# First feed-forward matrix by quarter blocks: seven products for eight, float32 gated values, and a second matrix that runs over eight PSUM banks

## Chip, cores and metric

The kernel runs on one core of a Trainium2 chip. The metric is the device time of one execution in microseconds (us), the median of several runs. TensorE (PE) multiplies, VectorE (DVE), ScalarE (ACT) and GpSimd (POOL) do elementwise work, and SyncE (SP) issues most of the DMAs. Operands lie in SBUF; PE writes to PSUM, which has eight banks of 128 x 512 float32.

## What is computed

One decoder layer on x of 512 tokens x 1024 features, all in float32. Three attention mixers are gated, merged, sent through `w_out` and added to x. Then comes the feed-forward block, which is what the change rewrites:

```python
h = _rms(x, norm2_g[layer])                                   # 512 x 1024
gate, up = jnp.split(h @ w_ffn_in[layer], 2, axis=-1)         # w_ffn_in 1024 x 5632
x = x + (jax.nn.silu(gate) * up) @ w_ffn_out[layer]           # w_ffn_out 2816 x 1024
```

## The kernel before

**Float32 products as three matmuls.** Every operand is split in two: `split` (L80) lets ACT round it to a "hi" part (L81) and DVE, or POOL where `eng` says so, subtract that from the operand to get a "lo" part (L82). `mm3` (L103) then issues hi x hi, hi x lo and lo x hi into one PSUM tile (L106 to L108). `weights` (L84) loads 256 KB blocks of a weight matrix through SP's queue into `raw` (five buffers), and splits each block into `whi` and `wlo` (six buffers each, of 128 x 512). It does this at high priority: the scheduler that sets the order on every engine places these instructions as early as buffers allow.

**Output projection (L1053 to L1080).** `w_out` is handled in four column blocks of 256; for each, four token tiles get eight `mm3`. DVE adds the PSUM tile to the residual `x2` (L1072). `x2`, four tiles of 512 KB, is loaded a second time from HBM for this (L1043). In the last column block, `norm_T` normalises each token tile, transposes it on PE and splits it to `xh2` and `xl2`.

**First feed-forward matrix (L1082 to L1129).** The loop over `c` goes through 11 chunks of 256 gate columns and the 256 up columns that go with them. In a chunk, each of two groups `j` of 128 columns gets eight `mm3` for gate and eight for up, with all 512 tokens as the moving operand: 2 x 2 x 8 x 3 = 96 matmuls of 128x512. The first chunk is done in halves of 256 tokens, since the last token tiles' norms are still under way. ACT takes the tanh (L1121), DVE multiplies twice (L1122, L1123), both times reading a PSUM tile, and the result is split at once to `hh` and `hl`.

**Second feed-forward matrix (L1130 to L1145).** Two halves of 512 output columns one after the other; in each, 22 blocks of 128 rows of `w_ffn_out` are multiplied with the 22 pairs `hh`, `hl` for four token tiles, in four PSUM banks. The last three blocks (`LAST`) are done tile by tile, so that the sums and the writes to HBM follow each other.

PSUM tiles `pf` of this part come from one pool of eight banks (`m2_tile`) in rotation.

Of the kernel before, what the change touches and what calls it, by code (L numbers as in the profile page):

```python
# [67 lines left out]
def block_kernel(ctx: ExitStack, tc: tile.TileContext, x, norm1_g, norm2_g, w_in, qk_norm_g, cmp_pos, cmp_w,  # L68
                 w_ba, w_bb, w_bc, w_out, w_fi, w_fo, rel_bias, onehot, masks, out):
    nc = tc.nc  # L70
    x, out = x[0], out[0]
    w_in, w_ba, w_bb, w_bc, w_out, w_fi, w_fo = (w[0] for w in (w_in, w_ba, w_bb, w_bc, w_out, w_fi, w_fo))
# [3 lines left out]
    wp = ctx.enter_context(tc.tile_pool(name="wts", bufs=6))  # L76
# [3 lines left out]
    def split(dst_hi, dst_lo, src, eng=None):  # L80
        nc.scalar.copy(dst_hi, src)  # L81
        (eng or nc.vector).tensor_tensor(out=dst_lo, in0=src, in1=dst_hi.bitcast(F32), op=ALU.subtract)  # L82

    def weights(w, segs, kcs, per=2, pool=()):  # L84

        res = {}
        width = sum(n for _, n in segs)
        with tc.high_priority():
            for k0 in kcs[::per]:
                raw = wp.tile([128, per, width], F32, name="raw", tag="raw", bufs=5)  # L90
                o = 0
                for c0, n in segs:
                    nc.sync.dma_start(raw[:, :, o:o + n],
                                      w[k0 * 128:(k0 + per) * 128, c0:c0 + n].rearrange("(k p) c -> p k c", p=128))
                    o += n
                hi = wp.tile([128, per, width], F32R, name="whi", tag="whi")
                lo = wp.tile([128, per, width], F32R, name="wlo", tag="wlo")
                split(hi, lo, raw, nc.gpsimd if pool and k0 // per % 4 in pool else None)
                for j in range(per):
                    res[k0 + j] = (hi[:, j, :], lo[:, j, :])  # L100
        return res

    def mm3(ps, pairs, k0=0, n=None):  # L103
        n = n or len(pairs)
        for j, ((ah, al), (bh, bl)) in enumerate(pairs, k0):
            nc.tensor.matmul(ps, ah, bh, start=(j == 0), stop=False)  # L106
            nc.tensor.matmul(ps, ah, bl, start=False, stop=False)  # L107
            nc.tensor.matmul(ps, al, bh, start=False, stop=(j == n - 1))  # L108
# [58 lines left out]
    def norm_T(xt, t, ss, n, g, xh, xl, pst, tmp, lo):  # L167
# [940 lines left out]
    for c in range(0, DFF, 256):
        if c:
            wg = weights(w_fi, [(c, 256)], list(range(KC)))  # L1110
            pgs = [m2_tile() for _ in range(2)]
# [4 lines left out]
        for j in range(2):
            pu = pus[j]
            if c:
                ffn_in(pu, wu, j)
            th = hp_.tile([128, S], F32, name="fth", tag="fth", bufs=2)  # L1120
            nc.scalar.activation(th, pgs[j], AF.Tanh, scale=0.5)  # L1121
# [8 lines left out]
    for c in range(0, D, 512):  # L1130
        pss = [m2_tile() for _ in range(NT)]
        wk = {}
        for k in range(NF):
            wk.update(weights(w_fo, [(c, 512)], [k], per=1))
            for t in range(NT if k < NF - LAST else 0):
                ts = slice(t * 128, (t + 1) * 128)
                mm3(pss[t], [((hh_[k][:, ts], hl_[k][:, ts]), wk[k])], k, NF)
        for t in range(NT):
            ts = slice(t * 128, (t + 1) * 128)
            mm3(pss[t], [((hh_[k][:, ts], hl_[k][:, ts]), wk[k]) for k in range(NF - LAST, NF)], NF - LAST, NF)  # L1140
            for q, dma in enumerate((nc.sync, nc.scalar)):
                cs = slice(256 * q, 256 * q + 256)
                xs = x2[t][:, c + 256 * q:c + 256 * q + 256]
                nc.vector.tensor_tensor(out=xs, in0=xs, in1=pss[t][:, cs], op=ALU.add)
# [20 lines left out]
```

## Time and profile before

| what | value |
|---|---|
| median of 3 runs | 999.03 us (994.99 to 999.38) |
| profiled execution | 995.54 us, span of its instructions 993.8 us |
| granted TensorE clock, mean | 0.993 |
| PE / DVE / ACT / POOL busy | 974.3 / 568.1 / 437.5 / 175.4 us |
| output projection | about 576 to 624 us of the span |
| first feed-forward matrix | about 624 to 867 us |
| second feed-forward matrix | about 867 us to the end |

The table's busy times are unions of the instructions' spans on each engine. Matmuls overlap in the pipeline, so a matmul's own duration is longer than the distance from its start to the next start; that distance is what a stream of matmuls costs. The stages follow each other on PE, so a stage's length is read off the first starts of its matmuls. From 648 us on POOL has no instruction.

### The profile page before, as it was taken

What the parts mean: (1) busy time and instruction counts of PE and PEld (TensorE: products, weight loads), DVE (VectorE), ACT (ScalarE), POOL (GpSimd) and SP (SyncE); (2) the same over time, 40 slices, a digit from 0 to 9 for tenths busy, and PEclk for the clock granted to TensorE, in tenths of its full rate; (3) what the DMA queues carried; (4) which work ended last, traced back from release to release, by engine and by line L of the source; (5) the groups of instructions that cost most, each with busy time, mean ns of one, the idle gap of its engine ahead of it and who ended that gap; (6) DMA issues with size and microseconds to landing.
All of it is one profiled execution on the core that took longest, in us unless ns stands there. A gap on an engine that the chain in (4) does not pass through costs nothing.

```text
span 993.8 us, 16076 instructions
## 1 busy us (share of the span) xinstructions
PE 974.3 (98%) x5887; PEld 827.0 (83%) x5887; DVE 568.1 (57%) x1277; ACT 437.5 (44%) x956; POOL 175.4 (18%) x156
## 2 busy tenths in 40 slices
PE   6999999999999999989999999999999999999998
PEld 6889999899887578858777899988888888888886
DVE  6699999766665655665764654544344444422321
ACT  5544555755665555554543434433233233322220
POOL 4135555543100202231110312000000000000000
PEclk9999999999999899989999999999999999999999
DMA  8541344433232334346613462233333323332421
GB/s 210 122 128 44 85 119 132 123 109 122 90 104 67 85 117 138 107 141 193 180 62 97 140 210 86 85 94 108 96 85 105 107 85 91 110 97 96 138 75 42
DMA packets 119264, 109.91 MB, mean 111 GB/s; under 512 B 19931, under 2 KB 105234, under 8 KB 119186
## 3 DMA queue, kind: packets, MB, share of 16 engines
q1 hardware_dynamic: 116994, 107.85, 37.4%
q10 hardware_dynamic: 2192, 1.05, 0.4%
q8 instruction: 46, 0.75, 0.3%
q14 instruction: 32, 0.26, 0.1%
HBM read 96.66 MB, written 12.21 MB: 110 GB/s over the span
## 4 chain that ended last, share of the span: by engine, by line
PE 96%; DMA 1%; DVE 1%; ACT 1%; issue 0%; SPq 0%; DVEq 0%; ACTq 0%
PE pf L108 14%; PE pf L107 14%; PE pf L106 14%; PE pm L107 13%; PE pm L106 13%; PE pm L108 13%; PE tr L111 5%; PE ovb L541 2%; PE lg L363 2%; PE lg L364 2%; PE ova L541 1%; PE lg L843 1%; DMA raw<-in_w_in 1%; PE ovc L888 1%; PE lg L838 0%
## 5 line engine op out<-in xcount | busy, mean ns | idle before, releaser
L82 DVE TENSOR_TENSOR wlo<-raw,whi 128x512 fp32r<-128x512 f32 (+1 forms) x243 | 182.5, 756 | 147.7 <-ACT whi L81 146.6
L81 ACT CAST whi<-raw 128x512 fp32r<-128x512 f32 (+1 forms) x288 | 176.8, 619 | 173.9 <-PE pf L108 78.6
L107 PE MATMUL pm<-wlo,xh 128*128 128x256 f32 (+1 forms) x512 | 145.9, 288 | 0.3 <-DVE wlo L82 0.3
L108 PE MATMUL pm<-whi,xl 128*128 128x256 f32 (+1 forms) x512 | 145.3, 286 | 0.5 <-POOL xl L82 0.5
L106 PE MATMUL pm<-whi,xh 128*128 128x256 f32 (+1 forms) x512 | 145.7, 289 | 0.0
L107 PE MATMUL pf<-xl,whi 128*128 128x512 f32 (+1 forms) x384 | 142.6, 372 | 0.1
L106 PE MATMUL pf<-xh,whi 128*128 128x512 f32 (+1 forms) x384 | 142.5, 372 | 0.0
L108 PE MATMUL pf<-xh,wlo 128*128 128x512 f32 (+1 forms) x384 | 142.0, 371 | 0.0
L107 PEld LDWEIGHTS pm<-wlo,xh 128*128 128x128 f32 x512 | 98.5, 193 | 1.9 <-issue 0.8
L108 PEld LDWEIGHTS pm<-whi,xl 128*128 128x128 f32 x512 | 98.7, 193 | 1.4 <-POOL xl L82 0.8
L106 PEld LDWEIGHTS pm<-whi,xh 128*128 128x128 f32 x512 | 98.3, 194 | 0.4
L107 PE MATMUL pm<-xl,whi 128*128 128x512 f32 x224 | 88.8, 396 | 0.0
L108 PE MATMUL pm<-xh,wlo 128*128 128x512 f32 x224 | 88.6, 395 | 0.0
L106 PE MATMUL pm<-xh,whi 128*128 128x512 f32 x224 | 88.4, 395 | 0.0
L107 PEld LDWEIGHTS pf<-xl,whi 128*128 128x128 f32 x384 | 72.3, 188 | 12.8 <-DVE xl L82 0.3
L108 PEld LDWEIGHTS pf<-xh,wlo 128*128 128x128 f32 x384 | 72.2, 188 | 12.6
L106 PEld LDWEIGHTS pf<-xh,whi 128*128 128x128 f32 x384 | 72.2, 188 | 12.3
L82 POOL TENSOR_TENSOR wlo<-raw,whi 128x512 fp32r<-128x512 f32 x45 | 62.2, 1402 | 111.6 <-ACT whi L81 100.8
L106 PE MATMUL pf<-whi,hh 128*128 128x512 f32 x176 | 69.4, 395 | 0.0
L108 PE MATMUL pf<-whi,hl 128*128 128x512 f32 x176 | 69.4, 395 | 0.0
L107 PE MATMUL pf<-wlo,hh 128*128 128x512 f32 x176 | 69.4, 395 | 0.0
L562 ACT ACTIVATE p<-p,m 128x128 f32<-128x128 f32 (+3 forms) x96 | 53.9, 562 | 28.6 <-DVE m L547 26.4
(312 smaller groups left out, 1702.3 us busy)
## 6 DMA issues: line engine op xcount, KB each, us to landing
raw<-in_w_in SPq DMA_DIRECT2D x92, 256.0 KB, 3.0
raw<-in_w_ffn_in SPq DMA_DIRECT2D x88, 256.0 KB, 2.9
raw<-in_w_ffn_out SPq DMA_DIRECT2D x44, 256.0 KB, 2.8
raw<-in_w_in SPq DMA_DIRECT2D x52, 128.0 KB, 2.4
x<-in_x SPq DMA_DIRECT2D x8, 512.0 KB, 5.9
tab<-dvec SPq DMA_DIRECT2D x16, 256.0 KB, 3.3
dz<-tz SPq DMA_DIRECT2D x16, 256.0 KB, 2.4
tz<-dz SPq DMA_DIRECT2D x16, 256.0 KB, 3.3
```

The source lines that it names most:

```text
L81: nc.scalar.copy(dst_hi, src)
L82: (eng or nc.vector).tensor_tensor(out=dst_lo, in0=src, in1=dst_hi.bitcast(F32), op=ALU.subtract)
L106: nc.tensor.matmul(ps, ah, bh, start=(j == 0), stop=False)
L107: nc.tensor.matmul(ps, ah, bl, start=False, stop=False)
L108: nc.tensor.matmul(ps, al, bh, start=False, stop=(j == n - 1))
L111: nc.tensor.transpose(dst, src, ident[0:src.shape[0], 0:src.shape[0]])
L363: nc.tensor.matmul(lg, qs, k[:, 0, 0:w], start=True, stop=False)
L364: nc.tensor.matmul(lg, qs, k[:, 1, 0:w], start=False, stop=stop)
L541: mm = nc.tensor.matmul(ov[64 * j:64 * j + 64, 128 * b:S], v(b), pts[j][:, 4 * b:3 * b + NT, :], start=first and b == 0, stop=last and b = ...
L562: nc.scalar.activation(p[:, 0:w], p[:, 0:w], AF.Exp, bias=m[:, 0:1], scale=-1.0, accum_out=m[:, 1:2])
L843: nc.tensor.matmul(lg[32 * r:32 * r + 32, c:c + n], ld["q", g][hp, 128 * i + 32 * r:128 * i + 32 * r + 32], ld["k", g][hp, 128 * r:128 * r ...
L888: nc.tensor.matmul(ov[h, 128 * b_:128 * q1], ld["v", 0][:, b_, h], d["pt", jj][:, 2 * b_:b_ + q1, :], start=b_ == 0, stop=False)
```

## The change

The chunks after the first are computed by quarter blocks with a Strassen scheme in Winograd's form. For a chunk, the weight block is cut in four: `a11` (upper 512 rows, gate columns), `a21` (upper rows, up columns), `a12` (lower rows, gate), `a22` (lower rows, up), each of two 128 x 512 tiles. The normalised input is cut in four by feature half and token half. Seven products of such quarters, with sums of quarters as operands, replace eight.

- `norm_T` also copies the normalised input in float32 to `xf` (ACT, 128x512, eight times). Four differences of its quarters (`t1` to `t4`, 128 x 1024 each) are made on DVE and split, once.
- Weight blocks go through SP to a pool of their own, `fraw` (twelve buffers). The sums `s1` to `s4` are made on POOL, eight adds of 128x512 a chunk, in `fsum` or in place. Seven operands of two tiles are split, fourteen tiles a chunk in place of eight; POOL subtracts two of the lo parts, DVE twelve.
- A product is 2 x 4 x 3 = 24 matmuls of 128x256. A chunk has 7 x 24 = 168 of them, in place of 96 of 128x512.
- Products are summed outside PSUM: one ACT copy and seven DVE adds of a PSUM tile to a float32 tile in SBUF (`ea`, `eu1`, `eu2`, `ec22`). `swiglu` then reads SBUF alone, where the two multiplies read PSUM before.
- The gated values stay in float32 (`hid`) and are split only in the second matrix, block by block. There the row block is the outer loop and both column halves run together over eight banks.

```diff
+    xf = np_.tile([128, KC, S], F32, name="xf")          # norm_T: nc.scalar.copy(xf[:, 4*q:4*q+4, ts], ps)
...
+    for name, out_, p, q in (("t1", f11, f12, f11), ("t3", f12, f22, f12), ("t2", f22, f22, f11), ("t4", f21, f21, f22)):
+        th_, tl_ = (tp.tile([128, HK, S // 2], F32R, name=f"x{name}{v}") for v in "hl")
+        nc.vector.tensor_tensor(out=out_, in0=p, in1=q, op=ALU.subtract)
+        split(th_, tl_, out_)
+        xb[name] = (th_, tl_)
...
+    def swiglu(dst, g, u):
+        th = ep.tile([128, 512], F32, name="fth", tag="fth", bufs=2)
+        nc.scalar.activation(th, g, AF.Tanh, scale=0.5)
+        nc.vector.scalar_tensor_tensor(out=th, in0=th, scalar=1.0, in1=g, op0=ALU.add, op1=ALU.mult)
...
+        nc.vector.scalar_tensor_tensor(out=dst, in0=th, scalar=0.5, in1=u, op0=ALU.mult, op1=ALU.mult)
...
+    def fi_operands(c):
+        fr = {}
+        with tc.high_priority():
+            for r, (n, k) in enumerate((("a11", 0), ("a21", 0), ("a22", HK), ("a12", HK))):
+                for h in range(2):
+                    t_ = ep.tile([128, 2, 256], F32, name="fraw", tag="fraw", bufs=12)
+                    k0, c0 = k + 2 * h, c + (DFF if n[1] == "2" else 0)
+                    nc.sync.dma_start(t_, w_fi[k0 * 128:k0 * 128 + 256, c0:c0 + 256].rearrange("(k p) c -> p k c", p=128))
+                    fr[n, h] = t_
+        def add(n, dst, p, q, op):
...
+                nc.gpsimd.tensor_tensor(out=fr[n, h], in0=fr[p, h], in1=fr[q, h], op=op)
+        def get(n):
+            with tc.high_priority():
+                if n == "s2":
+                    add("s1", None, "a21", "a22", ALU.add)
+                    add("s2", None, "s1", "a11", ALU.subtract)
+                elif n == "s3":
+                    add("s3", "a21", "a11", "a21", ALU.subtract)
+                elif n == "s4":
+                    add("s4", "s2", "a12", "s2", ALU.subtract)
+                res = []
+                for h in range(2):
+                    hi = wp.tile([128, 2, 256], F32R, name="whi", tag="whi")
+                    lo = wp.tile([128, 2, 256], F32R, name="wlo", tag="wlo")
+                    split(hi, lo, fr[n, h], nc.gpsimd if (n, h) in (("a22", 1), ("s1", 1)) else None)
+                    res += [(hi[:, j, :], lo[:, j, :]) for j in range(2)]
+            return res
...
+    for c in range(256, DFF, 256):
+        get = fi_operands(c)
...
+        for a, b in (("a11", "b11"), ("s2", "t2"), ("a12", "b21"), ("s3", "t3"), ("s1", "t1"), ("a22", "t4"), ("s4", "b22")):
+            w, (bh, bl) = get(a), xb[b]
+            ps = m2_tile()
             for j in range(2):
+                cs = slice(128 * j, 128 * j + 128)
+                mm3(ps[:, 256 * j:256 * j + 256], [((w[k][0][:, cs], w[k][1][:, cs]), (bh[:, k, :], bl[:, k, :]))
+                                                   for k in range(HK)])
+            if a == "a11":
+                nc.scalar.copy(ev["a"], ps)
+            elif a == "s2":
+                add_ps("u1", "a", ps)          # nc.vector.tensor_tensor(out=ev[dst], in0=ev[src], in1=ps, op=ALU.add)
...
+            elif a == "s1":
+                add_ps("c22", "u2", ps)
+                add_ps("u1", "u1", ps)
+            elif a == "a22":
+                add_ps("u2", "u2", ps)
+                swiglu(h3[:, :, lo_t], ev["a"], ev["u2"])
+            else:
+                add_ps("u1", "u1", ps)
+                swiglu(h3[:, :, hi_t], ev["u1"], ev["c22"])
...
+    for k in range(NF):
+        for c in range(2):
+            wk[k, c] = weights(w_fo, [(512 * c, 512)], [k], per=1)[k]
+        hk[k] = [hs_.tile([128, S], F32R, name=f"hs{v}", tag=f"hs{v}", bufs=4) for v in "hl"]
+        split(*hk[k], hid[k // 2][:, k % 2, :])
+        if k < NF - LAST:
+            for c in range(2):
+                for t in range(NT):
+                    fo(k, c, t)                # mm3(pss[c][t], ...)
```

**DVE in a middle chunk.** Before, a chunk has fourteen DVE instructions, eight `wlo`, two `hl` and four multiplies (L1122, L1123) with a PSUM tile `pf` among their sources. Seven of its rows:

```order
L82 TENSOR_TENSOR wlo_8317<-raw_8314,whi_8316 128x512
L82 TENSOR_TENSOR wlo_8323<-raw_8320,whi_8322 128x512
L82 TENSOR_TENSOR wlo_8395<-raw_8392,whi_8394 128x512
L82 TENSOR_TENSOR wlo_8401<-raw_8398,whi_8400 128x512
L1122 SCALAR_TENSOR_TENSOR fth_8384<-fth_8384,pf_8253 128x512
L1123 SCALAR_TENSOR_TENSOR fth_8352<-fth_8352,pf_8326 128x512
L82 TENSOR_TENSOR hl6_8357<-fth_8352,hh6_8356 128x512
```

Now a chunk has twenty-three. The same engine, a middle chunk (`eu1` and the like are the float32 sums, `h4` a gated tile):

```order
L82 TENSOR_TENSOR wlo_8912<-fraw_8781,whi_8911 128x512
L82 TENSOR_TENSOR wlo_8942<-fsum_8829,whi_8941 128x512
L1182 TENSOR_TENSOR eu1_8792<-ea_8791,pf_8845 128x512
L82 TENSOR_TENSOR wlo_8977<-fraw_8783,whi_8976 128x512
L1182 TENSOR_TENSOR ea_8791<-ea_8791,pf_8879 128x512
L1130 SCALAR_TENSOR_TENSOR fth_9010<-fth_9010,ea_8791 128x512
L82 TENSOR_TENSOR wlo_9017<-fsum_8833,whi_9016 128x512
L1182 TENSOR_TENSOR eu2_8793<-eu1_8792,pf_8915 128x512
L82 TENSOR_TENSOR wlo_9021<-fsum_8835,whi_9020 128x512
L82 TENSOR_TENSOR wlo_9075<-fraw_9054,whi_9074 128x512
L1182 TENSOR_TENSOR ec22_8794<-eu2_8793,pf_8949 128x512
L1182 TENSOR_TENSOR eu1_8792<-eu1_8792,pf_8949 128x512
```

Sixteen of the twenty-three (twelve `wlo`, four multiplies) now read two SBUF tiles; the seven L1182 rows read one PSUM tile.

**POOL in a middle chunk.** Before it had no row in this part of the program. Now ten stand there for each chunk, here with sums of the next chunk ahead of lo parts of this one:

```order
L1155 TENSOR_TENSOR fsum_9108<-fraw_9058,fraw_9062 128x512
L1155 TENSOR_TENSOR fsum_8833<-fraw_8787,fsum_8833 128x512
L1155 TENSOR_TENSOR fraw_9058<-fraw_9054,fraw_9058 128x512
L1155 TENSOR_TENSOR fsum_9110<-fraw_9060,fraw_9064 128x512
L1155 TENSOR_TENSOR fsum_8835<-fraw_8789,fsum_8835 128x512
L1155 TENSOR_TENSOR fraw_9060<-fraw_9056,fraw_9060 128x512
L82 TENSOR_TENSOR wlo_8946<-fsum_8831,whi_8945 128x512
L1155 TENSOR_TENSOR fsum_9112<-fsum_9108,fraw_9054 128x512
L1155 TENSOR_TENSOR fsum_9114<-fsum_9110,fraw_9056 128x512
L82 TENSOR_TENSOR wlo_8981<-fraw_8785,whi_8980 128x512
```

**SP around the output projection.** Before, the residual's four loads follow the eleventh block of `w_out`:

```order
L93 DMA raw<-in_w_out 128x2x256 x6
L1043 DMA x_0_6960<-in_x 128x1024
L1043 DMA x_1_6961<-in_x 128x1024
L1043 DMA x_2_6962<-in_x 128x1024
L1043 DMA x_3_6963<-in_x 128x1024
L1049 DMA gb_6973<-in_norm_g 128x1024
L93 DMA raw<-in_w_out 128x2x256 x5
```

Now twelve loads of the feed-forward weights stand ahead of them:

```order
L93 DMA raw<-in_w_out 128x2x256 x6
L1146 DMA fraw<-in_w_ffn_in 128x2x256 x12
L93 DMA raw<-in_w_out 128x2x256
L1045 DMA x_0_6960<-in_x 128x1024
L93 DMA raw<-in_w_out 128x2x256 x2
L1045 DMA x_1_6961<-in_x 128x1024
L1045 DMA x_2_6962<-in_x 128x1024
L1045 DMA x_3_6963<-in_x 128x1024
L1051 DMA gb_6973<-in_norm_g 128x1024
```

One more block of `w_out` is loaded ahead of the first residual tile, and two between the first and the second.

**DVE around the residual.** Before, the lo parts for the last of the third column block (`wlo_7278`, `wlo_7284`) stand behind additions to tiles 0 to 2 of the residual:

```order
L1072 TENSOR_TENSOR x2_3_6963<-x2_3_6963,pf_7010 128x256
L82 TENSOR_TENSOR wlo_7272<-raw_7269,whi_7271 128x512
L1072 TENSOR_TENSOR x2_0_6960<-x2_0_6960,pf_7147 128x256
L1072 TENSOR_TENSOR x2_1_6961<-x2_1_6961,pf_7148 128x256
L1072 TENSOR_TENSOR x2_2_6962<-x2_2_6962,pf_7149 128x256
L82 TENSOR_TENSOR wlo_7278<-raw_7275,whi_7277 128x512
L82 TENSOR_TENSOR wlo_7284<-raw_7281,whi_7283 128x512
```

Now the same two (`wlo_7279`, `wlo_7285`) stand behind the first addition to tile 2, and the second of them behind the first to tile 3:

```order
L1075 TENSOR_TENSOR x2_1_6961<-x2_1_6961,pf_7009 128x256
L1075 TENSOR_TENSOR x2_1_6961<-x2_1_6961,pf_7149 128x256
L1075 TENSOR_TENSOR x2_2_6962<-x2_2_6962,pf_7010 128x256
L1075 TENSOR_TENSOR x2_2_6962<-x2_2_6962,pf_7150 128x256
L82 TENSOR_TENSOR wlo_7279<-raw_7276,whi_7278 128x512
L1075 TENSOR_TENSOR x2_3_6963<-x2_3_6963,pf_7011 128x256
L82 TENSOR_TENSOR wlo_7285<-raw_7282,whi_7284 128x512
```

The first addition to a tile is the one that needs its load to have landed; all four now come right before these lo parts.

The order up to the output projection is the same in both kernels but for line numbers.

More of the change, by code (lines that the diff above doesn't have):

```diff
@@ L190, in norm_T @@
             split(xh[:, 4 * q:4 * q + 4, ts], xl[:, 4 * q:4 * q + 4, ts], ps, eng=lo[q])
+            if xf is not None:
+                nc.scalar.copy(xf[:, 4 * q:4 * q + 4, ts], ps)
     ps1 = ExitStack()
@@ L1102, in block_kernel @@
         ffn_in(pus[j], wu, j, hi_t)
+    HK = KC // 2
+    tp = ctx.enter_context(tc.tile_pool(name="tsum", bufs=1, side="right", reuse_waits="tile"))
+    fx = ExitStack()
+    ep = fx.enter_context(tc.tile_pool(name="ev", bufs=1, side="right", reuse_waits="tile"))
+    xb = {"b11": (xh2[:, 0:HK, lo_t], xl2[:, 0:HK, lo_t]), "b21": (xh2[:, HK:KC, lo_t], xl2[:, HK:KC, lo_t]),
+          "b22": (xh2[:, HK:KC, hi_t], xl2[:, HK:KC, hi_t])}
+    f11, f12, f21, f22 = (xf[:, k, t] for k in (slice(0, HK), slice(HK, KC)) for t in (lo_t, hi_t))
@@ L1130, in block_kernel @@
[L1130 to L1137, printed above, removed]
+    hid = [hp_.tile([128, 2, S], F32, name=f"h{c}") for c in range(DFF // 256)]
+    def swiglu(dst, g, u):
+        th = ep.tile([128, 512], F32, name="fth", tag="fth", bufs=2)
+        nc.scalar.activation(th, g, AF.Tanh, scale=0.5)
+        nc.vector.scalar_tensor_tensor(out=th, in0=th, scalar=1.0, in1=g, op0=ALU.add, op1=ALU.mult)
+        if len(dst.shape) == 3:
+            th, u = (v.rearrange("p (j t) -> p j t", j=2) for v in (th, u))
+        nc.vector.scalar_tensor_tensor(out=dst, in0=th, scalar=0.5, in1=u, op0=ALU.mult, op1=ALU.mult)
@@ new lines, in block_kernel @@
+    for j in range(2):
+        swiglu(hid[0][:, j, :], pgs[j], pus[j])
+    def fi_operands(c):
[9 more added lines that the diff above has]
+            for h in range(2):
+                if dst is None:
+                    fr[n, h] = ep.tile([128, 2, 256], F32, name="fsum", tag="fsum", bufs=6)
+                else:
+                    fr[n, h] = fr[dst, h]
+                nc.gpsimd.tensor_tensor(out=fr[n, h], in0=fr[p, h], in1=fr[q, h], op=op)
[9 more added lines that the diff above has]
+                res = []
+                for h in range(2):
+                    hi = wp.tile([128, 2, 256], F32R, name="whi", tag="whi")
[3 more added lines that the diff above has]
+            return res
+        return get
@@ new lines, in block_kernel, with add_ps @@
+    for c in range(256, DFF, 256):
+        get = fi_operands(c)
+        ev = {n: ep.tile([128, 512], F32, name=f"e{n}", tag=f"e{n}", bufs=2)
+              for n in ("a", "u1", "u2", "c22")}
+        def add_ps(dst, src, ps):
+            nc.vector.tensor_tensor(out=ev[dst], in0=ev[src], in1=ps, op=ALU.add)
+        h3 = hid[c // 256]
+        for a, b in (("a11", "b11"), ("s2", "t2"), ("a12", "b21"), ("s3", "t3"), ("s1", "t1"), ("a22", "t4"), ("s4", "b22")):
+            w, (bh, bl) = get(a), xb[b]
+            ps = m2_tile()
+            for j in range(2):
+                cs = slice(128 * j, 128 * j + 128)
[5 more added lines that the diff above has]
+                add_ps("u1", "a", ps)
+            elif a == "a12":
+                add_ps("a", "a", ps)
+            elif a == "s3":
+                add_ps("u2", "u1", ps)
+            elif a == "s1":
[4 more added lines that the diff above has]
+                swiglu(h3[:, :, lo_t], ev["a"], ev["u2"])
+            else:
+                add_ps("u1", "u1", ps)
+                swiglu(h3[:, :, hi_t], ev["u1"], ev["c22"])
@@ new lines, in block_kernel, with fo @@
+    fx.close()
+    hs_ = ctx.enter_context(tc.tile_pool(name="hsp", bufs=1, reuse_waits="tile"))
+    pss = [[m2_tile() for _ in range(NT)] for _ in range(2)]
+    wk, hk = {}, {}
+    def fo(k, c, t):
+        ts = slice(t * 128, (t + 1) * 128)
+        mm3(pss[c][t], [((hk[k][0][:, ts], hk[k][1][:, ts]), wk[k, c])], k, NF)
+    for k in range(NF):
[7 more added lines that the diff above has]
+                    fo(k, c, t)
@@ L1138, in block_kernel @@
+    for c in range(2):
         for t in range(NT):
             ts = slice(t * 128, (t + 1) * 128)
-            mm3(pss[t], [((hh_[k][:, ts], hl_[k][:, ts]), wk[k]) for k in range(NF - LAST, NF)], NF - LAST, NF)
+            for k in range(NF - LAST, NF):
+                fo(k, c, t)
             for q, dma in enumerate((nc.sync, nc.scalar)):
                 cs = slice(256 * q, 256 * q + 256)
-                xs = x2[t][:, c + 256 * q:c + 256 * q + 256]
-                nc.vector.tensor_tensor(out=xs, in0=xs, in1=pss[t][:, cs], op=ALU.add)
-                dma.dma_start(out[ts, c + 256 * q:c + 256 * q + 256], xs)
+                xs = x2[t][:, 512 * c + 256 * q:512 * c + 256 * q + 256]
+                nc.vector.tensor_tensor(out=xs, in0=xs, in1=pss[c][t][:, cs], op=ALU.add)
+                dma.dma_start(out[ts, 512 * c + 256 * q:512 * c + 256 * q + 256], xs)
```

28 lines of the change are left out of this document (3 added, 25 removed).

## The prediction

> **What bounds the kernel now.** I read the page's busy times and its chain of waits first, to see which engine sets the end; then the stages' busy times; then the timeline of PE, for what a matmul of each width costs; then DVE and POOL, since the change gives both more to do.
>
> ```profile
> span 993.8 us, 16076 instructions
> PE 974.3 (98%) x5887; PEld 827.0 (83%) x5887; DVE 568.1 (57%) x1277; ACT 437.5 (44%) x956; POOL 175.4 (18%) x156
> PE 96%; DMA 1%; DVE 1%; ACT 1%; issue 0%; SPq 0%; DVEq 0%; ACTq 0%
> core 0: us, PE busy (x) PEld busy (x) DVE busy (x) ACT busy (x) POOL busy (x), PEclk, DMA share, GB/s
> 692.00:714.00 22.00, 22.00 (x99) 18.22 (x98) 9.41 (x14) 7.46 (x13) 0.00 (x0) 1.00 0.36 98
> ```
>
> PE is on 96% of the chain, and in the first feed-forward matrix it is always busy while DVE works 9.41 us of 22.00 and POOL nothing. So in this stage DVE and POOL can take more work for nothing, until one of them is full. What PE pays is the distance between starts:
>
> ```profile
> 589.37 0.28 PE L107 MATMUL pf<-wlo,zh 128*128 128x256 f32 x1
> ...
> 599.93 0.28 PE L108 MATMUL pf<-whi,zl 128*128 128x256 f32 x1
> 699.66 0.39 PE L108 MATMUL pf<-xh,wlo 128*128 128x512 f32 x1
> ...
> 703.97 0.39 PE L106 MATMUL pf<-xh,whi 128*128 128x512 f32 x1
> ```
>
> Between the first pair lie 88 steps: 10.56 / 88 = 0.120 us for a 128x256. Between the second lie 19: 4.31 / 19 = 0.2268 us for a 128x512. Two of 256 columns cost 0.240, 6% more than one of 512.
>
> **PE's part.** A chunk before is 96 x 0.2268 = 21.8 us. Now it is 168 x 0.120 = 20.2 us: of the 12.5% fewer products, 7% is left, 1.6 us a chunk or 16 us over ten chunks. This is the gain if all else keeps up.
>
> **DVE and POOL.** The rows for one instruction each:
>
> ```profile
> L82 DVE TENSOR_TENSOR wlo<-raw,whi 128x512 fp32r<-128x512 f32 x8 | 5.5, 692 | 3.6 <-ACT whi L81 3.6
> 598.58 1.29 DVE L82 TENSOR_TENSOR wlo<-raw,whi 128x512 fp32r<-128x512 f32 x2 [1.15 <-ACT whi L81]
> 67.28 1.29 POOL L82 TENSOR_TENSOR wlo<-raw,whi 128x512 fp32r<-128x512 f32 x1
> 67.46 1.65 DVE L82 TENSOR_TENSOR wlo<-raw,whi 128x512 fp32r<-128x512 f32 x1
> 68.52 1.74 POOL L82 TENSOR_TENSOR wlo<-raw,whi 128x512 fp32r<-128x512 f32 x1
> 342.01 1.23 POOL L557 TENSOR_TENSOR tabm<-tab,topm 128x512 f32<-128x512 f32 x1
> 342.12 0.68 DVE L973 SCALAR_TENSOR_TENSOR tz<-tz,pm 128x512 f32<-128x512 f32 x1
> L981 DVE SCALAR_TENSOR_TENSOR zl<-tz,zh 128x512 fp32r<-128x512 f32 x8 | 6.5, 825 | 2.7 <-ACT zh L980 2.6
> ```
>
> A DVE instruction of 512 columns takes 0.69 us, and two in a row 1.29, so each costs its queue 0.60. Alone, the twenty-three of a new chunk are 23 x 0.60 = 13.8 us, and POOL's ten are 10 x 1.29 = 12.9 us. Both would fit under 20.2.
>
> They do not run alone. At 67.46 DVE starts a `wlo` while POOL works on another. It takes 1.65 us and ends at 69.11, 0.55 us after POOL ends at 68.57: it stood still until POOL was done. POOL's next starts at 68.52 and takes 1.74 in place of 1.29: now it waited for DVE. So the two take turns, whole instruction by whole instruction, one pair per 1.29 + 0.45 - 0.05 = 1.70 us. The multiply at 342.12 reads a PSUM tile and one SBUF tile: it takes its 0.68 us under a running POOL instruction, with no delay. The `zl` multiply (two SBUF tiles, mean 825 ns against 0.69) shows that SCALAR_TENSOR_TENSOR is no exception. What counts is two SBUF sources.
>
> [...]
>
> The change makes ten POOL instructions a chunk where there were none, and gives DVE sixteen with two SBUF sources (twelve `wlo`; four `swiglu` multiplies, which read PSUM before). In the order POOL's ten stand in runs with all they need loaded, so in a run each waiting DVE instruction pays 1.70 - 0.60 = 1.10 us more. If none of the ten falls beside a PSUM add, a chunk of DVE is 13.8 + 10 x 1.10 = 24.8 us. If each of the seven adds hides under one, 24.8 - 7 x 0.60 = 20.6. Going through the two rows in order, POOL's run of six sums meets only one add (`eu1` after `wlo`), the run at `s2` another; I count eight full pairs and two that an add halves: 13.8 + 8 x 1.10 + 2 x 0.5 = 23.6 us. That is over PE's 20.2, so DVE sets the pace and PE waits for `wlo` about 3.4 us a chunk. Against 21.8 this is +1.8 us. The first and the last of the ten I put at PE's 20.2: for the first, POOL has made sums while the unchanged chunk runs; for the last, six of POOL's ten are left. Sum: 8 x 1.8 - 2 x 1.6 = **+11.2 us**. Bounds: PE's pace in all ten, -16; 24.8 in eight, 8 x 3.0 - 3.2 = +20.8.
>
> **ACT.** Fourteen casts, a copy and two tanh a chunk:
>
> ```profile
> L81 ACT CAST whi<-raw 128x512 fp32r<-128x512 f32 x128 | 79.5, 621 | 131.4 <-PE pf L108 74.0 <-PE pf L107 48.1 <-DVE x L1144 6.4
> L1121 ACT ACTIVATE fth<-pf 128x512 f32<-128x512 f32 x22 | 13.1, 595 | 45.0 <-PE pf L108 45.0
> L299 DVE TENSOR_TENSOR cqk_tm<-cqk_tm,rst 128x1024 f32<-128x1024 f32 x6 | 7.3, 1223 | 1.4 <-POOL rst L151 1.3
> ```
>
> 17 x 0.62 = 10.5 us, half a chunk: hidden.
>
> **The first chunk.** Its 96 products' worth of PE work stays. New are eight `xf` copies (8 x 0.62 = 5.0 us ACT) and four differences with four lo parts of 1024 columns (8 x 1.22 = 9.8 us DVE). DVE was busy 9.41 of 22 in a like chunk, and two `hl` of 0.69 go: 9.8 + 8 fits in 24, beside matmuls. But the split of the last token tiles, for which PE waits at this place, shares ACT with the copies: **+0.5 us**, about one copy, between 0 and +3, five of them.
>
> **The output projection.** Twelve `fraw` loads now stand in SP's queue ahead of the residual's.
>
> ```profile
> 570.00 8.59 SPq L93 DMA_DIRECT2D raw<-in_w_out  x6
> 578.64 1.88 SPq L1043 DMA_DIRECT2D x<-in_x  x4
> 585.47 14.20 SPq L93 DMA_DIRECT2D raw<-in_w_out  x5
> x<-in_x SPq DMA_DIRECT2D x8, 512.0 KB, 5.9
> 444.00:448.00 4.00, 3.84 (x16) 2.63 (x15) 3.78 (x7) 3.24 (x7) 1.29 (x1) 1.00 0.85 237
> ```
>
> The residual's loads were issued at 578.64 and took some 6 us. Twelve loads are 3.1 MB, 13 us at the 237 GB/s that a full stretch moves; the residual is 2.1 MB more, 9 us; and its tiles 1 to 3 now follow `w_out` loads that were issued after 585.47. So tile 3 lands about 602 to 604. DVE's `wlo` for the third column block, due near 601, stands behind the additions to tiles 1 to 3. I take **+3 us**; 0 if the DMAs move faster, +6 if the last addition waits to 604 and ACT's sums of squares queue behind.
>
> **Between the matrices.** Before, the first `hh` was split long before the second matrix began. Now the split of `hid` stands in ACT's row right behind the last chunk's tanh, which waits for DVE's add of PE's last product: 0.6 + 0.6 + 0.62 us and handovers, **+2.5 us**, between 0 and +4.
>
> **The second matrix.** The same 528 matmuls; two weight tiles and one split per block are 3 x 0.6 = 1.8 us of DVE beside 24 x 0.2268 = 5.4 us of PE (matmuls of the same shape): hidden. The tail is the same: 0.
>
> **Sum.** 3.0 + 0.5 + 11.2 + 2.5 = +17.2 us on the profiled execution's own 995.54: 1012.7. That run lies 3.5 us under the median of 999.03 and inside its runs; between the two bases I predict 1014.
>
> **The rivals.** *PE's pace (faster).* If POOL's instructions get in DVE's way less than at 67 us, DVE is done in 20.2 and PE sets the chunk: 995.5 + 3.0 + 0.5 - 16 + 2.5 = 985.5. It decides below (20.2 - 13.8) / 10 = 0.64 us for each POOL instruction in place of 1.10. POOL's own delay, 0.45, is under that; DVE's, 1.65 - 0.69 = 0.96 even for a late starter, is over. Chance 0.12.
>
> *In between.* The adds hide more than I count, at 21.6 a chunk: 8 x -0.2 - 3.2 = -4.8, with the others +1.2 us: 997 to 1000, no change. Chance 0.10.
>
> *A slower clock besides.* PE idles in pieces of up to 3 us a chunk.
>
> ```profile
> 432.00:436.00 4.00, 0.51 (x4) 0.49 (x3) 4.00 (x5) 0.26 (x2) 3.18 (x4) 0.70 0.24 68
> 436.00:440.00 4.00, 3.27 (x15) 2.44 (x15) 2.20 (x8) 3.05 (x8) 0.00 (x0) 0.50 0.31 91
> ```
>
> After about 3.5 us of idling the granted clock stood at 0.50 for 4 us. If each chunk's wait did that, PE would lose 2 us of its 3.4 us slack, and where the loss falls on a late product perhaps 1 us would show: 1023. Chance 0.13. [...]
>
> **How the numbers follow.** The forecast has 0.65. A change of 0.5% (5 us) is about what a measurement of this kernel can tell from none. Slower than that: 0.65 + 0.13 = 0.78; the same: 0.10; faster: 0.12. The range leaves out PE's pace and the tops of the terms: from 997, the in-between case, to 1028, near 995.5 + 3 + 0.5 + 20.8 + 2.5 = 1022 and its 1 us a chunk. The forecast's own range is 1007 to 1022.
>
> **What would show it.** Right: in a middle chunk DVE is busy nearly all the time, its `wlo` rows have a mean over 1 us, POOL's sums about 1.6 us, and PE waits for `wlo` once or twice, mostly at the `s3` product; a chunk takes 23 to 24 us. The L1182 rows stay at 0.69. The residual's additions begin after 590, and the third column block starts late. Wrong: `wlo` at 0.69 beside POOL, a chunk of 20 to 21 us with PE unbroken, or PE's clock below 1 through the stage.

## Result and profile after

The changed kernel takes 1010.08 us (median of four runs, 1006.45 to 1011.75); the kernel before, run beside it, 997.01 (994.91 to 999.38). The ratio is 1.014, with a 95% interval of 1.0113 to 1.0167: slower by 13 us, where +15 us (1014) was forecast. The profiled execution took 1006.45 us; its span is 10.9 us longer than the one of before. It is the fastest of the four, with a mean granted clock of 0.991 against 0.986 in the others (1008.52 to 1011.75), so the traces account for 10.9 of the 13 us.

The page's lines on span, busy times and chain of waits, after:

```profile
span 1004.7 us, 17979 instructions
PE 963.8 (96%) x6607; PEld 850.4 (85%) x6607; DVE 715.4 (71%) x1395; ACT 480.8 (48%) x1038; POOL 339.2 (34%) x256
PE 81%; DVE 5%; POOL 4%; issue 4%; DMA 3%; ACT 1%; SPq 1%; DVEq 0%; POOLq 0%; ACTq 0%
```

PE works 10.5 us less than before and carries 81% of the chain, not 96%; DVE and POOL now carry 9% of it, where it was 1%. The busy time by chunk shows where. Each row runs from one chunk's ACT copy `ea<-pf` to the next; the columns are those of the prediction's windows (PE, weight loads, DVE, ACT, POOL, clock, DMA):

```profile
674.10:699.50 25.40, 23.22 (x193) 22.81 (x192) 24.70 (x24) 9.86 (x18) 20.12 (x13) 1.00 0.33 93
699.50:721.70 22.20, 19.19 (x146) 18.78 (x145) 21.40 (x24) 9.58 (x18) 15.04 (x10) 0.92 0.30 85
...
650.20:875.50 225.30, 208.54 (x1682) 205.06 (x1680) 217.60 (x230) 97.12 (x170) 152.66 (x92) 0.98 0.29 81
```

In these two middle chunks DVE is idle 0.7 and 0.8 us. How long the chunks are is read better on PE, by the second product of each, whose matmuls read `xt2h` (eight in each chunk; the line has the shortest, median and longest duration in ns, the first and the last start):

```profile
L106 PE MATMUL pf<-xt2h,whi x80: 277/280/284, 653.1 to 861.0; 128*128 128x256 f32 x80
```

From the first of these matmuls in one chunk to the first in the next, the first chunk lasts 19.9 us and the next eight 23.2 on average (21.1 to 25.6); that leaves 19.9 for the last. All ten (the row 650.20:875.50) take 225.3 us; the ten before took 217.6 without a pause on PE:

```profile
649.60:867.20 217.60, 217.60 (x966) 180.31 (x965) 95.29 (x143) 72.98 (x123) 0.00 (x0) 1.00 0.35 99
```

DVE's groups in 674 to 860 us (eight chunks), each with count, sum and mean in ns:

```profile
L82 DVE TENSOR_TENSOR wlo<-fraw,whi 128x512 fp32r<-128x512 f32 x55 | 71.0, 1291 | 0.2
L82 DVE TENSOR_TENSOR wlo<-fsum,whi 128x512 fp32r<-128x512 f32 x40 | 35.4, 886 | 0.0
L1182 DVE TENSOR_TENSOR eu<-eu,pf 128x512 f32<-128x512 f32 x31 | 20.9, 673 | 0.0
L1130 DVE SCALAR_TENSOR_TENSOR fth<-fth,eu 128x512 f32<-128x512 f32 x8 | 14.3, 1781 | 0.0
L1133 DVE SCALAR_TENSOR_TENSOR h<-fth,ec 128x512 f32<-128x512 f32 x8 | 14.2, 1773 | 0.0
L1130 DVE SCALAR_TENSOR_TENSOR fth<-fth,ea 128x512 f32<-128x512 f32 x8 | 13.3, 1658 | 5.6 <-ACT fth L1129 5.6
L1133 DVE SCALAR_TENSOR_TENSOR h<-fth,eu 128x512 f32<-128x512 f32 x8 | 8.7, 1090 | 0.0
```

Every group with two SBUF sources is longer than 0.69 us; the add that reads a PSUM tile has 0.673. What is over 0.68 each in the six groups with two SBUF sources sums up to 33.6 + 8.2 + 8.8 + 8.7 + 7.8 + 3.3 = 70.4 us, 8.8 us a chunk. A run of POOL's sums beside DVE shows each instruction's own wait (start, duration):

```profile
678.18 1.74 POOL L1155 TENSOR_TENSOR fsum<-fraw,fsum 128x512 f32<-128x512 f32 x1
679.87 1.74 POOL L1155 TENSOR_TENSOR fraw<-fraw 128x512 f32<-128x512 f32 x1
678.69 1.78 DVE L82 TENSOR_TENSOR wlo<-fraw,whi 128x512 fp32r<-128x512 f32 x1
680.39 1.77 DVE L82 TENSOR_TENSOR wlo<-fsum,whi 128x512 fp32r<-128x512 f32 x1
682.08 0.68 DVE L1182 TENSOR_TENSOR eu<-ea,pf 128x512 f32<-128x512 f32 x1
682.68 1.18 DVE L82 TENSOR_TENSOR wlo<-fraw,whi 128x512 fp32r<-128x512 f32 x1
```

Both rows advance by 1.70 us an instruction, DVE alone would by 0.60. POOL's first here ends at 679.92, DVE's `wlo` of 678.69 at 680.47, 0.55 later. The PSUM add at 682.08 runs under POOL; the `wlo` behind it waits only for what is left of POOL's instruction, 0.50 us more than alone. PE pays at the `wlo` operands of its products; the view of the tile `pf` in the ten chunks lists for what it sat idle (us, times):

```profile
  DVE wlo L82: 29.4, 23
  POOL wlo L82: 7.3, 7
```

This view adds up matmuls and weight loads, which wait at the same time; PE itself is idle for 225.3 - 208.5 = 16.8 us of the ten chunks.

### The profile page after: what moved, and what is told of

The parts are those of the page before. It is cut to its first block, busy times and chain, and to the rows that moved or that the text cites. A ratio compares the mean times of both kernels' runs of the same rounds, so it can differ in the third digit from the quotient of the medians.

```text
span 1004.7 us, 17979 instructions
## 1 busy us (share of the span) xinstructions
PE 963.8 (96%) x6607; PEld 850.4 (85%) x6607; DVE 715.4 (71%) x1395; ACT 480.8 (48%) x1038; POOL 339.2 (34%) x256
## 4 chain that ended last, share of the span: by engine, by line
PE 81%; DVE 5%; POOL 4%; issue 4%; DMA 3%; ACT 1%; SPq 1%; DVEq 0%; POOLq 0%; ACTq 0%
PE pm L107 13%; PE pm L108 13%; PE pm L106 13%; PE pf L108 10%; PE pf L106 9%; PE pf L107 9%; PE tr L111 5%; DVE wlo L82 2%; PE ovb L543 2%; PE lg L365 2%; PE lg L366 2%; POOL fsum L1155 2%; POOL fraw L1155 1%; POOL wlo L82 1%; DMA fraw<-in_w_ffn_in 1%
## 5 line engine op out<-in xcount | busy, mean ns | idle before, releaser
L82 DVE TENSOR_TENSOR wlo<-raw,whi 128x512 fp32r<-128x512 f32 (+1 forms) x163 | 128.5, 793 | 73.7 <-ACT whi L81 72.9
L81 ACT CAST whi<-raw 128x512 fp32r<-128x512 f32 (+1 forms) x208 | 127.3, 617 | 86.0 <-PE pf L108 39.3
L82 DVE TENSOR_TENSOR wlo<-fraw,whi 128x512 fp32r<-128x512 f32 x70 | 86.5, 1239 | 0.2
L106 PE MATMUL pf<-xh,whi 128*128 128x256 f32 x304 | 86.0, 284 | 0.1
L108 PE MATMUL pf<-xh,wlo 128*128 128x256 f32 x304 | 85.8, 284 | 0.2 <-DVE wlo L82 0.2
L107 PE MATMUL pf<-xl,whi 128*128 128x256 f32 x304 | 86.0, 283 | 0.0
L106 PE MATMUL pf<-whi,hsh 128*128 128x512 f32 x176 | 69.4, 395 | 2.4 <-ACT hsh L81 2.4
L107 PE MATMUL pf<-wlo,hsh 128*128 128x512 f32 x176 | 69.4, 395 | 0.0
L108 PE MATMUL pf<-whi,hsl 128*128 128x512 f32 x176 | 68.3, 395 | 0.0
L564 ACT ACTIVATE p<-p,m 128x128 f32<-128x128 f32 (+3 forms) x96 | 53.9, 561 | 28.5 <-DVE m L549 26.4
L1155 POOL TENSOR_TENSOR fsum<-fraw 128x512 f32<-128x512 f32 x20 | 36.9, 1849 | 80.8 <-DMA fraw<-in_w_ffn_in 57.4
```

Of the source, the lines that this page charges most:

```text
L564: nc.scalar.activation(p[:, 0:w], p[:, 0:w], AF.Exp, bias=m[:, 0:1], scale=-1.0, accum_out=m[:, 1:2])
L1155: nc.gpsimd.tensor_tensor(out=fr[n, h], in0=fr[p, h], in1=fr[q, h], op=op)
```

## Experiments

The theory: POOL and DVE exclude each other for whole instructions whenever the one of DVE reads two SBUF tiles, as in the rows from 678 us (1.70 us a pair), so POOL's ten instructions of a chunk cost DVE more than they spare it, and DVE sets the pace. The rivals: DVE simply has too many instructions; POOL is a slow supplier; narrow matmuls or the clock hold PE.

**All on DVE.** POOL's ten instructions of a chunk are moved to DVE.

```diff
-                nc.gpsimd.tensor_tensor(out=fr[n, h], in0=fr[p, h], in1=fr[q, h], op=op)
+                nc.vector.tensor_tensor(out=fr[n, h], in0=fr[p, h], in1=fr[q, h], op=op)
...
-                    split(hi, lo, fr[n, h], nc.gpsimd if (n, h) in (("a22", 1), ("s1", 1)) else None)
+                    split(hi, lo, fr[n, h], None)
```

> POOL's ten instructions of a chunk (eight sums, two lo parts) go to DVE; the rest is as in the changed kernel. Turn-taking theory: with POOL silent no DVE instruction pays 1.10 us; DVE has 33 x 0.60 = 19.8 us a chunk, under PE's 20.2, so a middle chunk falls from 23.2 to about 20.3 us and the time to 980 to 988 us, under the kernel before. Rival, DVE is simply given too much: ten more instructions on the fullest engine make a chunk longer than 23.2 us and the time longer than 1010. Rival, 256-wide matmuls or a lower clock keep PE from 20.2: a chunk stays at about 23 us with DVE idle in it.

Measured: 982.92 us, ratio to the kernel before 0.9871 (0.9838 to 0.9904), as forecast. The ten chunks:

```profile
651.30:851.50 200.20, 200.20 (x1683) 199.71 (x1681) 194.29 (x320) 101.73 (x170) 0.00 (x0) 1.00 0.31 91
```

DVE's largest group, 680 to 830 us:

```profile
L82 DVE TENSOR_TENSOR wlo<-fraw,whi 128x512 fp32r<-128x512 f32 x60 | 39.8, 684 | 1.7 <-ACT whi L81 1.5
```

DVE does ten instructions more in each chunk and is done sooner; `wlo` is back at 0.684 us and PE is idle for no part of the ten chunks. The count of DVE's instructions was not the limit, and neither the 256-wide matmuls nor the clock kept PE from 20 us a chunk. DVE is close behind, with 194 of 200 us in use.

**Idle POOL.** The same, and POOL makes ten additions a chunk that nobody reads.

```diff
+        hb = hid[c // 256 - 1]
+        for _ in range(10):
+            nc.gpsimd.tensor_tensor(out=spare, in0=hb[:, 0, :], in1=hb[:, 1, :], op=ALU.add)
```

> As the run with all sums on DVE, and POOL does in each middle chunk ten additions of two finished blocks of hid into a tile that nobody reads; no other instruction waits for them. Turn-taking theory: DVE pays for POOL's work though it has no use for it: 33 x 0.60 + 10 x 1.10 = 30.8 us a chunk less what the seven PSUM adds hide, 26 to 30 us, 1045 to 1085 us in all. Rival, POOL is slow as a supplier (its sums come late, and DVE and PE wait for those): with nobody waiting for POOL, the same time as the run with all sums on DVE, 980 to 990.

Measured: 1057.58 us, ratio 1.0627 (1.0583 to 1.0671), as forecast. The ten chunks:

```profile
653.90:917.00 263.10, 225.53 (x1683) 216.79 (x1681) 262.34 (x314) 101.65 (x170) 171.97 (x91) 0.92 0.23 67
```

One group of DVE, and POOL's, 680 to 830 us:

```profile
L82 DVE TENSOR_TENSOR wlo<-fraw,whi 128x512 fp32r<-128x512 f32 x46 | 43.2, 961 | 0.0
L1181 POOL TENSOR_TENSOR spare<-h 128x512 f32<-128x512 f32 x50 | 93.4, 1869 | 59.3 <-DVE h L1133 55.8
```

Ten POOL instructions that supply nothing make the ten chunks 62.9 us longer and DVE busy all the time (262.3 of 263.1 us). So POOL's mere work costs DVE time, and a slow supplier is not needed to explain the loss; in the changed kernel some of PE's waits did end with a lo part that POOL made (7.3 us in the view above), and what those add was not separated. The eight middle chunks are 26.9 us on average, 6.8 more than in the run with all on DVE, or 0.68 us for each POOL instruction and not 1.10. That is what the prediction's sum gives when all seven PSUM adds hide 0.60: 10 x 1.10 - 7 x 0.60 = 6.8.

**No sums.** The eight sums are left out, raw blocks stand in for them; POOL keeps two lo parts.

```diff
-                nc.gpsimd.tensor_tensor(out=fr[n, h], in0=fr[p, h], in1=fr[q, h], op=op)
+                fr[n, h] = fr[p, h]
```

> The eight sums of weight blocks are left out of the computation (raw blocks stand in for s1 to s4); POOL keeps its two lo parts, DVE its twenty-three instructions, PE its 168 products. Turn-taking theory: 13.8 + 2 x 1.10 = 16.0 us of DVE, PE sets the pace at 20.1 us, 980 to 986 us. Rival, DVE's count of twenty-three: nothing changes for DVE, a chunk stays at 23 us, 1005 to 1010. Its time is also the floor for any way of making the sums.

Measured: 977.99 us, ratio 0.9828 (0.9792 to 0.9863), 2 us under the forecast; a chunk:

```profile
674.10:694.00 19.90, 19.90 (x169) 19.90 (x169) 16.66 (x26) 11.36 (x19) 2.58 (x2) 1.00 0.35 106
```

PE's pace, as the theory has it: the twenty-three DVE instructions alone do not fill a chunk (16.66 us of DVE, 16.0 forecast). The sums' cost in the changed kernel, some 30 us, comes from where they run: with all on DVE they cost about 5 by the medians.

**Two lo parts on POOL.** The sums on DVE, two lo parts left to POOL.

```diff
-                nc.gpsimd.tensor_tensor(out=fr[n, h], in0=fr[p, h], in1=fr[q, h], op=op)
+                nc.vector.tensor_tensor(out=fr[n, h], in0=fr[p, h], in1=fr[q, h], op=op)
```

> The eight sums go to DVE, the two lo parts of a22 and s1 stay on POOL. Turn-taking theory: 31 x 0.60 + 2 x 1.10 = 20.8 us of DVE a chunk, 985 to 990 us, some 4 us more than with all ten on DVE: a POOL instruction saves DVE 0.60 and costs it 1.10. Rival, relief: each instruction given to POOL takes 0.60 off DVE, so 1 us a chunk less or the same as with all ten on DVE.

Measured: 981.93 us, ratio 0.9861 (0.9823 to 0.9899), not to be told from all on DVE. The forecast missed: its 4 us more did not come, and the time is the rival's. POOL's two instructions and DVE beside them:

```profile
717.40 2.74 POOL L82 TENSOR_TENSOR wlo<-fsum,whi 128x512 fp32r<-128x512 f32 x1 [15.18 <-ACT whi L81]
720.68 1.77 POOL L82 TENSOR_TENSOR wlo<-fraw,whi 128x512 fp32r<-128x512 f32 x1 [0.54 <-ACT whi L81]
718.31 0.68 DVE L1130 SCALAR_TENSOR_TENSOR fth<-fth,eu 128x512 f32<-128x512 f32 x1
718.91 0.68 DVE L1182 TENSOR_TENSOR eu<-ea,pf 128x512 f32<-128x512 f32 x1
719.51 1.18 DVE L82 TENSOR_TENSOR wlo<-fsum,whi 128x512 fp32r<-128x512 f32 x1
...
721.21 1.78 DVE L1133 SCALAR_TENSOR_TENSOR h<-fth,ec 128x512 f32<-128x512 f32 x1
```

The first POOL instruction ends at 720.14; with 1.29 us of its own it began to work at about 718.85, when DVE came to its PSUM add. Until then DVE's instructions with two SBUF sources kept it out, the last the multiply at 718.31. It then costs DVE 0.50, the second 1.10: 31 x 0.60 + 1.6 = 20.2 us, and not 20.8; PE's chunks take 19.9 on average. My price of 1.10 for each was too high for an instruction that comes alone.

**One SBUF source on POOL.** As the idle additions, but POOL reads one tile.

```diff
-            nc.gpsimd.tensor_tensor(out=spare, in0=hb[:, 0, :], in1=hb[:, 1, :], op=ALU.add)
+            nc.gpsimd.tensor_scalar(out=spare, in0=hb[:, 0, :], scalar1=1.0, scalar2=EPS, op0=ALU.mult, op1=ALU.add)
```

> As the run with idle POOL adds, but POOL's ten instructions of a chunk read one SBUF tile and not two (a multiply and add with constants). If any POOL instruction that reads SBUF shuts out DVE's two-source ones for its whole length, DVE's rows again show 1.1 us more beside each (less, if the POOL instruction is shorter), and the time is 1025 to 1065 us. Rival, only two sources on both sides collide: DVE's rows stay at 0.68 and the time is that of all sums on DVE, 980 to 985.

Measured: 993.87 us, ratio 0.9991 (0.9978 to 1.0005), between the two forecasts. POOL's instructions after the chunks, where DVE is idle (shortest, median and longest in ns):

```profile
L1181 POOL TENSOR_SCALAR spare<-h x14: 620/621/934, 855.3 to 864.8; 128x512 f32<-128x512 f32 x14
```

One of them beside a PSUM add of DVE, and DVE's row at the second matrix:

```profile
711.91 7.14 POOL L1181 TENSOR_SCALAR spare<-h 128x512 f32<-128x512 f32 x1
718.45 0.72 DVE L1186 TENSOR_TENSOR eu<-ea,pf 128x512 f32<-128x512 f32 x1
865.42 2.54 DVE L82 TENSOR_TENSOR hsl<-h,hsh 128x512 fp32r<-128x512 f32 x4 [9.66 <-POOL spare L1181]
```

A chunk:

```profile
692.50:712.70 20.20, 20.20 (x173) 20.20 (x172) 20.20 (x35) 10.45 (x19) 19.54 (x9) 1.00 0.36 105
```

They do collide: an instruction of 0.62 us takes 7.14, and ends when DVE's PSUM add of 718.45 has let it in. In most chunks it is POOL that pays so, because 0.62 us just fits under one PSUM add (0.60 from start to start): the eight middle chunks are 20.2 us on average, 20.1 without POOL. Where the two take turns, DVE pays as well; in the chunk from 732.50 to 753.40, which took 20.90 us:

```profile
734.38 0.94 POOL L1181 TENSOR_SCALAR spare<-h 128x512 f32<-128x512 f32 x1
735.40 0.93 POOL L1181 TENSOR_SCALAR spare<-h 128x512 f32<-128x512 f32 x1
734.76 1.09 DVE L82 TENSOR_TENSOR wlo<-fraw,whi 128x512 fp32r<-128x512 f32 x1
735.77 1.09 DVE L1155 TENSOR_TENSOR fsum<-fraw,fsum 128x512 f32<-128x512 f32 x1
```

Both rows advance by 1.02 us, so a DVE instruction pays 0.42. A pair took 1.70 where POOL read two tiles; the 0.68 between them is the difference of POOL's own times, 1.29 - 0.62 = 0.67. So one SBUF source on POOL's side is enough for the collision, as the first theory said, and its price goes with the length of POOL's instruction. The time of 1025 to 1065 did not come, since POOL was mostly kept out. Most of the other 11 us is the row at 865.42: POOL had a backlog, and the split of `hid` waited for it.

**Idle POOL in the kernel before.** Ten such two-source additions in each of the ten later chunks of the kernel before.

```diff
+            for _ in range(10):
+                nc.gpsimd.tensor_tensor(out=spare, in0=hh_[-2].bitcast(F32), in1=hh_[-1].bitcast(F32), op=ALU.add)
             wg = weights(w_fi, [(c, 256)], list(range(KC)))
```

> The kernel before, with ten POOL adds of two finished hidden tiles in each of its ten later chunks into a tile that nobody reads. Turn-taking theory: DVE pays up to 10 x 1.10 = 11 us a chunk, but it has 9.4 of 21.8 us in use, so it still ends first and the time stays at 993 to 1000 us while DVE's wlo rows rise to 1.3 to 1.8 us. Rival, the delay itself reaches PE wherever a lo part is late by 1.1 us: a few us a chunk, 1010 to 1030.

Measured: 994.15 us, ratio 1.0004 (0.9991 to 1.0017). Its `wlo` group between 660 and 840 us:

```profile
L82 DVE TENSOR_TENSOR wlo<-raw,whi 128x512 fp32r<-128x512 f32 x65 | 61.5, 945 | 21.1 <-ACT whi L81 20.6
```

A chunk:

```profile
700.00:721.76 21.76, 21.76 (x98) 18.02 (x97) 11.36 (x14) 7.22 (x13) 14.72 (x11) 1.00 0.33 96
```

`wlo` goes from 0.69 to 0.945 us on average, less than the 1.3 to 1.8 forecast; PE does not notice. With DVE at half load (11.36 us of 21.76), the collision is free.

**Fillers against the clock.** In the trace of after the clock falls to 0.50 for 3.4 us in three chunks, each time behind a wait of 2.38 or 2.39 us such as the second of these (bracket: idle time and what ended it):

```profile
702.47 0.38 PE L108 MATMUL pf<-xt3h,wlo 128*128 128x256 f32 x1 [0.63 <-DVE wlo L82]
...
705.82 0.39 PE L108 MATMUL pf<-xt3h,wlo 128*128 128x256 f32 x1 [2.39 <-DVE wlo L82]
```

The changed kernel, with eight matmuls more where PE waits:

```diff
+                        for _ in range(8):
+                            nc.tensor.matmul(ps[:, 0:256], ah, bl_, start=False, stop=False)
                         nc.tensor.matmul(ps[:, 0:256], al, bh_, start=False, stop=False)
```

> The changed kernel with eight more products of 0.12 us in each s3 product, in the 2.5 us in which PE waits for wlo (they add one hi-lo term eight times more to the sum, so this part of the output is another); DVE, ACT and POOL have the same rows in the same order. If DVE alone sets the chunk, PE has 3 us of slack, the 1 us is free and the time stays at 1008 to 1012, with the clock at 1.00 through the chunks. If the three (in other runs perhaps six) falls of the clock to 0.50 cost 1 to 1.7 us each, the breaks of 1.5 us that are left don't cause them and the time falls to 1002 to 1007. If PE's own work set the chunk, ten times 1 us more: 1018 to 1020.

Measured: 1010.13 us, ratio 1.0159 (1.0143 to 1.0176); the changed kernel's interval, 1.0113 to 1.0167, overlaps it. The time is the one forecast for DVE alone setting the chunk. The ten chunks:

```profile
650.70:877.50 226.80, 213.21 (x1763) 209.93 (x1762) 217.79 (x229) 97.39 (x170) 154.17 (x93) 1.00 0.27 81
```

The mean clock of the stage is 1.00, where it was 0.98 in the row 650.20:875.50 above. DVE has the same work (217.8 and 217.6 us), and the stage is no shorter (226.8 and 225.3 us), though the falls are gone and PE had some 10 us more to do. So DVE sets the pace, and no cost of the falls shows here: PE catches up in its slack. A cost of the falls and one of the fillers that cancel each other to within 1.5 us are not excluded by this run alone.

**Handover.** All on DVE, with fewer buffers, so that the first `hs` tiles have room beside the chunks' own.

```diff
-                    t_ = ep.tile([128, 2, 256], F32, name="fraw", tag="fraw", bufs=12)
+                    t_ = ep.tile([128, 2, 256], F32, name="fraw", tag="fraw", bufs=10)
...
-                    fr[n, h] = ep.tile([128, 2, 256], F32, name="fsum", tag="fsum", bufs=6)
+                    fr[n, h] = ep.tile([128, 2, 256], F32, name="fsum", tag="fsum", bufs=4)
...
-        hk[k] = [hs_.tile([128, S], F32R, name=f"hs{v}", tag=f"hs{v}", bufs=4) for v in "hl"]
+        hk[k] = [hs_.tile([128, S], F32R, name=f"hs{v}", tag=f"hs{v}", bufs=3) for v in "hl"]
```

> All sums and lo parts on DVE, and fewer buffers (fraw 10, fsum 4, hs 3), so that the first hs tiles lie beside the chunks' own tiles and the first block of hid can be split while the chunks run. By the forecast's term for the handover, its 2.5 us goes: 978 to 982 us, 2 to 3 us under the run with all sums on DVE. Rival: the handover's wait is for PE's last product and not for the split, or loads of the smaller ring come late: no gain, 982 to 986.

Measured: 980.14 us, ratio 0.9855 (0.9832 to 0.9879). PE's rows where the matrices meet, in the changed kernel:

```profile
875.39 0.28 PE L108 MATMUL pf<-xh,wlo 128*128 128x256 f32 x1
878.04 0.50 PE L106 MATMUL pf<-whi,hsh 128*128 128x512 f32 x1 [2.36 <-ACT hsh L81]
```

and here:

```profile
851.68 0.28 PE L108 MATMUL pf<-xh,wlo 128*128 128x256 f32 x1
851.80 0.40 PE L106 MATMUL pf<-whi,hsh 128*128 128x512 f32 x1
```

The casts to `hsh` up to 860 us:

```profile
L81 ACT CAST hsh<-h x4: 617/622/623, 650.7 to 859.2; 128x512 fp32r<-128x512 f32 x4
```

The first cast to `hsh` now runs at 650.7 and the second matrix starts without a pause. Something else goes with the pause. In the run with all on DVE PE stood still as long here, and shortly after it the clock was at 0.50:

```profile
854.07 0.50 PE L106 MATMUL pf<-whi,hsh 128*128 128x512 f32 x1 [2.36 <-ACT hsh L81]
855.28:858.70 3.42, 3.42 (x9) 2.68 (x9) 2.60 (x5) 1.66 (x3) 0.00 (x0) 0.50 0.09 34
```

From its first matmul to the end the second matrix takes 128.2 us there and 126.5 here. In this stage PE sets the pace (busy in all of 854.10 to 978.50 there), and the difference is about what 3.4 us at half the clock lose. The trace shows the 2.5 us gone; the times cannot tell this version from the one with all on DVE, since their intervals overlap. It beats both kernels: 1.45% under the kernel before, by its interval 1.2 to 1.7%.

## Why the prediction was right

| term of the sum | forecast, us | profile against profile, us |
|---|---|---|
| output projection | +3.0 | 0 (47.8 to 47.8) |
| first chunk | +0.5 | +1.3 (25.1 to 26.4) |
| ten chunks | +11.2 | +7.7 (217.6 to 225.3) |
| between the matrices | +2.5 | +2.5 |
| second matrix, tail | 0 | 0 |
| sum | +17.2 | +11.5; less 0.7 of an earlier start, +10.9 (of unrounded terms) |

The stages run from the first start of their matmuls to the first start of the next stage's. The sum was 6 us too long; that 1014 lies only 4 us from the median is in part luck, since the median moved 2 us more than the profile.

- **The ten chunks**, the term that gave the sign. The mechanism, DVE standing behind POOL's sums for 1.10 us, is in the rows (678 to 683 us), and the runs with all on DVE and with idle POOL show it from both sides. The size was too large: I counted 8 x 1.10 + 2 x 0.5 = 9.8 us of waiting a chunk, the groups have 8.8. By DVE's rows from 674 to 860 us, 56 of the instructions with two SBUF sources are 0.9 to 1.1 us longer than 0.68 and 16 are 0.5 to 0.7 longer, so seven full waits a chunk and two half ones. Eight middle chunks of 23.2 us in place of 23.6 are 3.2 us of the difference, the first and the last at 19.9 in place of 20.2 most of the rest.
- **The output projection** is the mis-sized term. Its step was "13 us at the 237 GB/s that a full stretch moves". The DMAs moved far more in this stretch, and in the kernel before they already had (the last two columns are the DMA share and GB/s; a packet counts whole in the stretch in which it starts, so a share can pass 1); before:

```profile
580.00:585.00 5.00, 5.00 (x44) 5.00 (x43) 0.44 (x2) 0.81 (x2) 0.00 (x0) 1.00 1.03 353
```

After:

```profile
590.00:595.00 5.00, 5.00 (x44) 5.00 (x43) 0.94 (x3) 0.51 (x2) 3.83 (x3) 1.00 1.05 387
```

DVE's additions to the residual, the two to tile 0 and, by the order of DVE's instructions, the first to tile 3:

```profile
593.12 0.75 DVE L1075 TENSOR_TENSOR x<-x,pf 128x256 f32<-128x256 f32 x2 [2.93 <-DMA x<-in_x]
598.45 0.42 DVE L1075 TENSOR_TENSOR x<-x,pf 128x256 f32<-128x256 f32 x1
```

The additions do begin after 590, as forecast, but the one to tile 3 is done before 600, not at 602 to 604. The third column block does not start late, another sign that the prediction named: PE is busy in all of 590 to 600. The rate came from another stage, where the DMAs were busy 0.85 of the time, in place of this one's; why they moved less there was not tried.
- **The first chunk**: +1.3 lies inside 0 to +3. It is not POOL's: with all on DVE the same chunk takes 26.3 us (625.0 to 651.3). What in it costs the 1.3 us was not tried.
- **Between the matrices**: +2.5 as forecast, and the handover run takes it away. The chain is the forecast's: ACT's first cast to `hsh` starts at 877.38, right behind the last chunk's tanh at 876.85.
- **The rivals.** "PE's pace" gave 985.5; with the collision removed the kernel takes 982.9, so its sum was about right (the 3.0 of the output projection is too much in it, too) and only its condition was not met. "A slower clock besides" had falls of the clock right, in three chunks of ten and not in each; the run with fillers shows no price for them.

## What to carry to other kernels

An instruction moved from a busy VectorE to GpSimd can cost VectorE more than it spares it: here 0.60 us spared, up to 1.10 lost, and 1.014 of the time before became 0.987 by taking the work back. Before such a move, count VectorE's instructions with two SBUF sources in the same stretch and its slack there; with half its time free, in the kernel before, ten such additions a chunk cost nothing (ratio 1.0004). For a transfer, take the rate of the stretch where it will run (here 387 GB/s), not of another (237).

## What was not expected

- Which of the two engines goes first is not a plain alternation. In the run with one source, VectorE's row of two-source instructions kept GpSimd out until a PSUM add came: 7.14 us for a 0.62 us instruction. But in other stretches GpSimd got in after every single one of VectorE's (1.70 us a pair, or 1.02 with one source). A row of GpSimd instructions behind each other is not enough for that: the one of 7.14 us stood in such a row. In the rows with 1.78 us the turn passed to the other engine after each instruction; the 7.14 us show that the turn can also pass from one VectorE instruction to the next over a waiting GpSimd. What decides between the two was not tried.
- TensorE's clock fell to 0.50 behind a pause of 2.39 us; one of 0.63 us had ended 3.35 us before the end of that pause, with six matmuls between the two. In the run with all on DVE a single pause of 2.36 us behind unbroken work had a fall behind it as well, while a pause of the same 2.36 us in the changed kernel, at 878 us, had none. So a pause of this length can have a fall of the clock behind it, and does not always; what decides was not tried.
- GpSimd did a 128x512 with one source and two constants in 0.62 us, where one with two source tiles took 1.29 (`wlo` at 67.28 us in the kernel before).
